# New prices in the list scheduler of an encoder-layer kernel

## The chip, the cores and the metric

The kernel runs on one core of a Trainium2 chip, as one program. The metric is the device time of one execution in microseconds (us). A core has TensorE (PE, matrix products), VectorE (DVE), ScalarE (ACT), GpSimd (POOL) and a queue that issues transfers (SP). Each engine takes its own instructions strictly in the order in which the program was written, and waits on semaphores for the others.

## The reference

One layer of a bidirectional encoder is applied to two sequences of 256 tokens, width 2048, with the same weights. Both are handled together, as 512 columns.

```
mod = silu(c) @ w_ada + b_ada            # six parts: shift, scale, gate, twice
h   = (rms_norm(x) * (1 + sc1) + sh1) @ w_in
# RWKV-7 group: 16 heads of 64, scanned once forward and once backward
S = S * w_t + (S @ -kk_t) b_t^T + v_t k_t^T ;  y_t = S @ r_t
# short-conv group: h_b * conv3(h_c * h_x)
x = x + gt1 * (concat(y_rwkv, y_conv) @ w_out)
f = rms_norm(x) * (1 + sc2) + sh2
x = x + gt2 * ((silu(f @ w_gate) * (f @ w_up)) @ w_down)     # 5632 wide
y = rms_norm(x)
```

## The kernel before, in words

**Products.** Every large product is made in three passes for accuracy: a weight block of 128x1024 arrives by DMA (`w`, three buffers), ACT copies half of it, rounded, into a tile `h` (four buffers), DVE subtracts to get the rest (`split`), and PE then makes, for each 128x128 tile, three matmuls of 128x512: high by high, high by low, low by high (`products`). One such triple is one node of the scheduler. Rows of the profile for these read `b<-r,h` or `b<-g,h`. `stream` runs through the tiles of one product. All matmuls are issued at line 374, PE's transposes at line 385, ACT's copies and activations at line 392, DVE's two-operand products at line 401, its scalar-and-tensor ones at line 406, its scans at 425, its own transposes at 437, and every DMA at line 434.

**Stages.** In the head, a first part of the adaLN weights and of `w_in` is loaded and multiplied. Then follow eight head pairs `p`. For each, `pre(p)` normalises keys and makes the low-rank products, gates and two scans; `core(p)` does the recurrence in chunks of 64 tokens; `fin(p)` normalises the heads' output. The `w_in` products of the following pair, and DVE's adaLN sums for later parts (`aacc<-aw`, priority 8), are the work that lies beside it; during the last pair it is half of `w_out`. After the pairs come the other half of `w_out`, the gate and up products, the down products and the last norm, nearly all of it 128x512 matmuls.

**The gram stage.** `core(p)` begins with decays (ACT), eight DVE products, and then four groups of small products, one for each direction `d` and half `q`: eight products with 64 rows, 128 weight columns and 128 columns of data, into two PSUM banks; banks 2 and 3 for `q` = 0, 4 and 6 for `q` = 1, so the third group needs the banks of the first and the fourth those of the second. Each pair of banks is emptied by six ACT copies of 32 rows (three per bank) and four DVE products (two per bank, one on 64 rows and one on 128). Two engines do not touch one bank at a time: ACT takes the first bank while DVE takes the second, then they change over. PE's transposes follow, into banks 2 to 4, then a triangular solve on DVE (31 steps, with DVE transposes around it and 32x32 products behind it) and four chunk steps in which PE, ACT and DVE take turns.

**What sets the order.** The whole layer is first noted down as nodes (`Program.add`): an engine, a price in us, a priority (small is urgent: splits 0, evictions 1, core 2, fin 3, pre 4, small sums 5, adaLN 8, wide products 9) and the nodes it depends on. `schedule` then plays through time: the engine that can start first takes its most urgent ready node; a node is ready when the nodes it depends on have ended and a `latency` between the two engines has passed. For a DMA the planned landing is issue, 0.65, its bytes at 360 GB/s, and 0.8. PE's prices are stretched where the played clock is cold. Nodes are issued in the order of their planned starts. So prices decide only which instruction stands ahead of which on each engine's queue; the time is the chip's own.

Of the kernel before, what the change touches and what calls it, by code (L numbers as in the profile page):

```python
# [196 lines left out]
class Program:  # L197
    SAME = {"pe": 0.0, "act": 0.145, "dve": 0.13, "pool": 0.12, "sp": 0.0}

    @classmethod  # L200
    def latency(cls, a, b):

        if a == b:
            return cls.SAME[a]
        return 0.3 if b == "pe" else 0.2 if a == "pe" else 0.14

    def __init__(self):
        self.nodes = []
# [2 lines left out]
    def add(self, eng, dur, fn, reads, writes, prio, table=None, nbytes=0, rows=1.0):  # L211
        i = len(self.nodes)
        deps = set()
        todo = [(x, False) for x in reads] + [(x, True) for x in writes]
        for x, w in todo:
            if not isinstance(x, (V, ScratchView)):
                continue
            vt, p0, p1, m = x.region()
            s = vt.slot
            if s.cur is not vt:  # L220
                deps.update(n for n, *_ in s.acc)
                s.acc = []
                s.cur, s.base = vt, i
            if s.base is not None:
                deps.add(s.base)
            keep = []
            for e in s.acc:
                n, q0, q1, k, ew = e
                if (w or ew) and q0 < p1 and p0 < q1 and k & m or s.psum and n < i and self.nodes[n][0] != eng:
                    deps.add(n)  # L230
                if not (w and p0 <= q0 and q1 <= p1 and (k & m) == k):
                    keep.append(e)
            keep.append((i, p0, p1, m, w))
            s.acc = keep
        deps.discard(i)
        self.nodes.append([eng, dur, fn, deps, prio, table, nbytes, self.hold, rows])
        return i

    def schedule(self):
# [24 lines left out]
        while done < n:  # L264
            best = None
            for e in engines:
                t = free[e]
                while pend[e] and pend[e][0][0] <= t:
                    _, i = heapq.heappop(pend[e])
                    heapq.heappush(avail[e], (nodes[i][4], i))  # L270
                if avail[e]:
                    s = t
                elif pend[e]:
                    s = pend[e][0][0]
                else:
                    continue
                if best is None or s < best[0]:
                    best = (s, e)
            s, e = best
            free[e] = max(free[e], s)  # L280
            while pend[e] and pend[e][0][0] <= s:
                _, i = heapq.heappop(pend[e])
                heapq.heappush(avail[e], (nodes[i][4], i))
            if e == "dve" and avail[e][0][0] >= LOOK_PRIO and pend[e]:
                soon = [r for r, j in pend[e] if r <= s + LOOK and nodes[j][4] <= 2]
                if soon:
                    free[e] = min(soon)
                    continue
            _, i = heapq.heappop(avail[e])
            if e == "pe" and not nodes[i][5]:  # L290

                busy = [x for x in busy if x[1] > s - WINDOW]
                if sum((x[1] - max(x[0], s - WINDOW)) * x[2] for x in busy) < LEAST * WINDOW:
                    wides = [x for x in avail[e] if nodes[x[1]][5]]
                    if wides:
                        heapq.heappush(avail[e], (nodes[i][4], i))
                        avail[e].remove(min(wides))
                        heapq.heapify(avail[e])
                        i = min(wides)[1]
            eng, dur, fn, deps, prio, tb, nbytes = nodes[i][:7]  # L300
            start[i] = s
            if e == "act" and tb is not None and table["act"] not in tb:
                dur += 1.3
                table["act"] = tb[0]
            if e == "pe":
                dur += 0.085 * bool(tb and not wide)
                wide = tb
                busy.append((s, s + dur, nodes[i][8]))
                t = s
                k = int(t // CLOCK_WINDOW)  # L310
                while win < k:
                    cold = used < COLD if not cold else used < HOT
                    win, used = win + 1, 0.0
                rest = dur
                while rest > 1e-9:
                    f = 2.0 if cold else 1.0
                    e2 = min(t + rest * f, (win + 1) * CLOCK_WINDOW)
                    used += (e2 - t) * nodes[i][8] / CLOCK_WINDOW
                    rest -= (e2 - t) / f
                    t = e2  # L320
                    if rest > 1e-9:
                        cold = used < COLD if not cold else used < HOT
                        win, used = win + 1, 0.0
                dur = t - s
            free[e] = s + dur
            end = s + dur
            if nbytes:
                dma_free = max(dma_free, end + 0.65) + nbytes / 360e3
                end = dma_free + 0.8
            order.append(i)  # L330
            done += 1
            for j in succ[i]:
                ready_at[j] = max(ready_at[j], end + self.latency(e, nodes[j][0]))
                left[j] -= 1
                if left[j] == 0:
                    heapq.heappush(pend[nodes[j][0]], (ready_at[j], j))
# [11 lines left out]
def hymba_layer_kernel(ctx: ExitStack, tc: tile.TileContext, xT, par, cst, w_ada0, w_ada1, w_in0, w_in1,  # L348
# [6 lines left out]
    def pe(mms, prio, after=()):  # L355


        def price(m):
            cols, n = m[1].idx.size, m[3]
            if m[6]:  # L360
                return max(cols / 1200.0, n / 2375.0)
            if cols > 64:
                return max(0.218, n / 597.0)
            if cols > 32:
                return max(0.081, 0.0277 + n / 1200.0)
            return max(0.037, 0.0205 + n / 2400.0, min(0.056, 0.03 + n / 2400.0))

        cost = sum(price(m) for m in mms)

        rows = sum((1 if m[6] else 4) * m[3] / 2400.0 * (m[1].p1 - m[1].p0) * m[1].idx.size  # L370
                   for m in mms) / (16384 * cost)

        def fn():
            return [nc.tensor.matmul(R(out), lhsT=R(l), rhs=R(r), start=start, stop=stop)  # L374
                    for out, l, r, n, start, stop, one in mms]
        add("pe", cost, fn, [m[1] for m in mms] + [m[2] for m in mms] + list(after), [m[0] for m in mms], prio,
            table=mms[0][6],
            rows=rows)
# [4 lines left out]
    def tr(items, prio):  # L383
        def fn():
            return [nc.tensor.transpose(R(out), R(i), R(idn)) for out, i, idn in items]  # L385
        add("pe", (0.003 + items[0][0].idx.size / 1200.0) * len(items), fn,
            [i[1] for i in items] + [items[0][2]], [i[0] for i in items], prio)

    def act(out, in_, func, n, prio, scale=1.0, bias=0.0):
        ex = [x for x in (scale, bias) if isinstance(x, V)]  # L390
        add("act", (0.05 if in_.vt.slot.psum else 0.095) + n / 1200.0 + 0.09 * len(ex),
            lambda: nc.scalar.activation(out=R(out), in_=R(in_), func=func, scale=R(scale), bias=R(bias)),  # L392
            [in_] + ex, [out], prio, table=TABLES.get(func))

# [2 lines left out]

    def tt(out, a, b, op, n, prio, eng="dve"):
        e = nc.vector if eng == "dve" else nc.gpsimd
        add(eng, 0.07 + n / 960.0 if eng == "dve" else 0.1 + n / 445.0,  # L400
            lambda: e.tensor_tensor(out=R(out), in0=R(a), in1=R(b), op=op), [a, b], [out], prio)  # L401

    def stt(out, a, s, b, op0, op1, n, prio, eng="dve"):
# [5 lines left out]
    def ts(out, a, s1, op0, n, prio, s2=None, op1=None, fast=True, eng="dve"):  # L409
        e = nc.vector if eng == "dve" else nc.gpsimd  # L410

        def fn():
            if s2 is None:
                return e.tensor_scalar(out=R(out), in0=R(a), scalar1=R(s1), scalar2=None, op0=op0)
            return e.tensor_scalar(out=R(out), in0=R(a), scalar1=R(s1), scalar2=R(s2), op0=op0, op1=op1)
        cost = 0.07 + n / (1920.0 if fast else 960.0) if eng == "dve" else 0.1 + n * 0.0036
        cost += 0.06 * (isinstance(s1, V) + isinstance(s2, V))
        add(eng, cost, fn, [a, s1, s2], [out], prio)

    def recip(out, a, n, prio):  # L420
# [1 line left out]
            lambda: nc.vector.reciprocal(out=R(out), in_=R(a)), [a], [out], prio)  # L422

    def scan(out, m, x, prio):
        add("dve", 0.62, lambda: nc.vector.tensor_tensor_scan(
            out=R(out), data0=R(m), data1=R(x), initial=0.0, op0=ALU.mult, op1=ALU.add), [m, x], [out], prio)

    def pset(out, val, n, prio):
# [5 lines left out]
        add(eng, cost, lambda: e.dma_start(R(out), R(in_)), [in_, *after], [out], prio, nbytes=nbytes)  # L434

    def tr32(out, in_, n, prio):
        add("dve", 0.07 + n / 960.0, lambda: nc.vector.transpose(R(out), R(in_)), [in_], [out], prio)  # L437

    S_SPLIT, S_EVAC, S_CORE, S_FIN, S_PRE, S_MISC, S_ADA, S_MAIN = 0, 1, 2, 3, 4, 5, 8, 9
    S_HEAD, S_REV = 2, S_CORE  # L440
# [965 lines left out]
```

## Time and profile before

| | us |
|---|---|
| median of 3 runs (lowest, highest) | 2571.69 (2567.66, 2575.66) |
| the profiled execution's own time | 2574.54 |
| its span, first to last instruction | 2572.8 |
| PE, PE weight load, DVE, ACT, POOL busy | 2495.1, 1992.2, 1490.0, 981.9, 12.0 |
| share of the chain that ended last: PE, DVE, DMA, ACT | 85%, 5%, 4%, 3% |

The profiled execution is one execution of its own, so its time differs a little from the median of the runs. A busy PE is not a PE at its peak: matmuls overlap, and the mean of one (396 ns for a 128x512) is longer than its distance to the next. In a row of the groups there stand line, engine, operation, output and inputs, shapes, count, then busy time, mean ns of one, and the idle time of the engine just before, with what ended it. In a row of the waits there stand who waited, for whom, the total in us, how often, and the longest.

### The profile page before, as it was taken

The numbers are of one execution on the slowest core, as the hardware profiler recorded it, in microseconds if no ns is written. First come the engines' busy times: TensorE is split into PE (matmuls) and PEld (weight loads), VectorE is DVE, ScalarE is ACT, GpSimd is POOL, SyncE is SP. The second block draws the span as 40 slices with busy tenths as digits, with TensorE's granted clock in tenths as the row PEclk, the third lists the DMA queues.
The fourth block names the chain that finished last, engine by engine and source line by source line (L and its number), as shares of the span: only waits on it lengthen the run. The fifth ranks groups of instructions, "written<-read, shape, count | busy, mean of one in ns | idle before, by whom it ended". The sixth has DMA issues, their size and how long they took to land.

```text
span 2572.8 us, 38989 instructions
## 1 busy us (share of the span) xinstructions
PE 2495.1 (97%) x15292; PEld 1992.2 (77%) x15292; DVE 1490.0 (58%) x2840; ACT 981.9 (38%) x1772; POOL 12.0 (0%) x42
## 2 busy tenths in 40 slices
PE   6999999999999999999999999999999999999997
PEld 3567677777777777798888888888888888888887
DVE  4268888888989886988743333333333333333345
ACT  4374655746636543433222222222222222222232
POOL 0000000000000000000000000000000000000000
PEclk9999999999999999999999999999999999999999
DMA  9953534545435658536643333333333333333333
GB/s 339 349 152 117 148 113 139 147 130 147 145 113 152 217 152 289 181 106 189 186 128 96 99 98 93 96 99 98 94 95 98 99 97 93 97 98 99 97 92 107
DMA packets 149033, 352.74 MB, mean 137 GB/s; under 512 B 31984, under 2 KB 46704, under 8 KB 148848
## 3 DMA queue, kind: packets, MB, share of 16 engines
q1 hardware_dynamic: 148848, 350.24, 43.7%
q8 instruction: 120, 1.97, 0.3%
q14 instruction: 65, 0.53, 0.1%
HBM read 339.30 MB, written 12.45 MB: 137 GB/s over the span
## 4 chain that ended last, share of the span: by engine, by line
PE 85%; DVE 5%; DMA 4%; ACT 3%; issue 1%; SPq 0%; DVEq 0%; ACTq 0%
PE b L374 85%; ACT g L392 2%; DVE g L401 2%; DMA aw<-in_w_ada_dram 2%; DVE aacc L406 1%; DVE h L401 1%; DVE g L406 1%; DMA g<-hrmean 1%; PE b L385 1%; DMA w<-in_w_in_dram 1%; SPq L434 0%; DMA g<-hrpre 0%; ACT h L392 0%; DMA hrmean<-rowm 0%; DVE g L437 0%
## 5 line engine op out<-in xcount | busy, mean ns | idle before, releaser
L374 PE MATMUL b<-r,h 128*128 128x512 f32 x4872 | 1189.1, 396 | 6.6 <-DVE h L401 2.6
L374 PEld LDWEIGHTS b<-r,h 128*128 128x128 f32 x4872 | 901.8, 189 | 227.4 <-issue 27.8
L374 PE MATMUL b<-g,h 128*128 128x512 f32 x4460 | 1043.6, 391 | 0.0
L374 PEld LDWEIGHTS b<-g,h 128*128 128x128 f32 x4460 | 836.5, 188 | 188.8 <-issue 9.6
L401 DVE TENSOR_TENSOR h<-w,h 128x512 fp32r<-128x512 f32 (+3 forms) x795 | 539.7, 681 | 748.4 <-ACT h L392 743.1
L392 ACT ACTIVATE h<-w 128x512 fp32r<-128x512 f32 x787 | 492.4, 627 | 1259.6 <-PE b L374 1219.6
L406 DVE SCALAR_TENSOR_TENSOR aacc<-aw,sil,aacc 128x512 f32<-128x512 f32 x420 | 299.1, 746 | 64.4 <-DMA aw<-in_w_ada_dram 63.1
L401 DVE TENSOR_TENSOR g<-g,g 128x512 f32<-128x512 f32 (+25 forms) x699 | 257.2, 375 | 35.5 <-ACT g L392 15.1
L392 ACT ACTIVATE g<-b 32x128 f32<-32x128 f32 (+4 forms) x441 | 175.1, 401 | 123.2 <-PE b L374 93.1
L374 PEld LDWEIGHTS b<-g,g 128*64 128x64 f32 (+4 forms) x4104 | 160.8, 141 | 72.1 <-ACT g L392 31.1
L374 PE MATMUL b<-g,g 128*64 128x64 f32 (+4 forms) x4104 | 182.5, 230 | 23.8 <-ACT g L392 20.4
L392 ACT ACTIVATE g<-g 128x512 f32<-128x512 f32 (+4 forms) x190 | 113.8, 601 | 78.0 <-DVE g L401 61.5
L406 DVE SCALAR_TENSOR_TENSOR r<-b,md,r 128x256 f32<-128x256 f32 x192 | 85.9, 480 | 88.2 <-PE b L374 87.9
L401 DVE TENSOR_TENSOR g<-g,b 128x512 f32<-128x512 f32 x60 | 41.2, 687 | 60.4 <-PE b L374 60.3
L392 ACT ACT_TABLE_LOAD x54 | 69.3, 1283 | 2.0 <-PEq L1395 0.7
L374 PE MATMUL b<-g,sil 128*32 128x512 f32 (+1 forms) x352 | 40.2, 552 | 19.5 <-DMA g<-in_w_ada_dram 18.7
L401 DVE TENSOR_TENSOR g<-b,cs 64x256 f32<-64x256 f32 (+1 forms) x128 | 50.3, 416 | 3.5 <-ACT g L392 2.4
L392 ACT ACTIVATE g<-r 128x512 f32<-128x512 f32 (+1 forms) x40 | 21.6, 542 | 51.7 <-DVE r L406 41.3
L437 DVE STREAM_TRANSPOSE g<-g 128x512 f32<-128x512 f32 (+1 forms) x32 | 37.7, 1205 | 0.2
L374 PEld LDWEIGHTS b<-g,sil 128*32 128x32 f32 x352 | 8.4, 113 | 35.2 <-ACT g L392 17.9
L385 PE MATMUL b<-cs,g 128*128 128x128 f32 x160 | 26.7, 308 | 8.8 <-ACT g L392 4.9
L385 PEld LDWEIGHTS b<-cs,g 128*128 128x128 f32 x160 | 21.2, 159 | 17.0 <-ACT g L392 12.2
(83 smaller groups left out, 562.0 us busy)
## 6 DMA issues: line engine op xcount, KB each, us to landing
w<-in_w_gu_dram SPq DMA_DIRECT2D x176, 512.0 KB
aw<-in_w_ada_dram SPq DMA_DIRECT2D x224, 256.0 KB
w<-in_w_in_dram SPq DMA_DIRECT2D x102, 512.0 KB
w<-in_w_down_dram SPq DMA_DIRECT2D x88, 512.0 KB
g<-in_w_ada_dram SPq DMA_DIRECT2D x72, 512.0 KB
w<-in_w_out_dram SPq DMA_DIRECT2D x32, 512.0 KB
g<-in_xT_dram SPq DMA_DIRECT2D x8, 512.0 KB
r<-in_xT_dram SPq DMA_DIRECT2D x16, 256.0 KB
```

The source lines that it names most:

```text
L374: return [nc.tensor.matmul(R(out), lhsT=R(l), rhs=R(r), start=start, stop=stop) for out, l, r, n, start, stop, one in mms]
L385: return [nc.tensor.transpose(R(out), R(i), R(idn)) for out, i, idn in items]
L392: lambda: nc.scalar.activation(out=R(out), in_=R(in_), func=func, scale=R(scale), bias=R(bias)),
L401: lambda: e.tensor_tensor(out=R(out), in0=R(a), in1=R(b), op=op), [a, b], [out], prio)
L406: lambda: e.scalar_tensor_tensor(out=R(out), in0=R(a), scalar=R(s), in1=R(b), op0=op0, op1=op1),
L437: add("dve", 0.07 + n / 960.0, lambda: nc.vector.transpose(R(out), R(in_)), [in_], [out], prio)
```

## The change

Only prices and latencies of the scheduler are replaced. No instruction, tile, buffer, priority or dependency is touched.

```diff
 def latency(cls, a, b):
-    return 0.3 if b == "pe" else 0.2 if a == "pe" else 0.14
+    return 0.18 if b == "pe" else 0.2 if a == "pe" else 0.13
 # schedule(), a PE node; tb: it is a triple of wide passes, wide: so was the one before
-    dur += 0.085 * bool(tb and not wide)
+    dur += 0.1 * bool(wide and not tb)
 # price of one matmul: cols weight columns, n columns of data, m[6]: one pass
-    return max(cols / 1200.0, n / 2375.0)
+    return n / 2400.0 + 0.0133
 if cols > 64:
-    return max(0.218, n / 597.0)
+    return 0.124 if m[1].p1 - m[1].p0 <= 64 else max(0.218, n / 597.0)
+def held(out):
+    return 0.1 * (out.p1 - out.p0 < 128)
 # act: (0.05 from PSUM, 0.095 from SBUF) + n / 1200 + 0.09 per column operand
+    ... + held(out)
 # tt on DVE: 0.07 + n / 960;  ts: 0.07 + n / 1920 or n / 960, + 0.06 per column operand
+    ... + held(out)
 # scan
-    0.62
+    1.13
 # tr32, DVE's transpose of 32x32 blocks
-    0.07 + n / 960.0
+    0.37 if n == 256 else 0.05 + n / 560.0
```

The first applies to all engines: the time from the end of a node to the earliest start of one that depends on it. `held` adds 0.1 to ACT copies, DVE two-operand products and DVE scalar operations whose output has fewer than 128 rows.

More of the change, by code (lines that the diff above doesn't have):

```diff
@@ L387, in tr @@
             [i[1] for i in items] + [items[0][2]], [i[0] for i in items], prio)
+    def held(out):
+        return 0.1 * (out.p1 - out.p0 < 128)
     def act(out, in_, func, n, prio, scale=1.0, bias=0.0):
         ex = [x for x in (scale, bias) if isinstance(x, V)]
-        add("act", (0.05 if in_.vt.slot.psum else 0.095) + n / 1200.0 + 0.09 * len(ex),
+        add("act", (0.05 if in_.vt.slot.psum else 0.095) + n / 1200.0 + 0.09 * len(ex) + held(out),
             lambda: nc.scalar.activation(out=R(out), in_=R(in_), func=func, scale=R(scale), bias=R(bias)),
@@ L399, in tt @@
         e = nc.vector if eng == "dve" else nc.gpsimd
-        add(eng, 0.07 + n / 960.0 if eng == "dve" else 0.1 + n / 445.0,
+        add(eng, 0.07 + n / 960.0 + held(out) if eng == "dve" else 0.1 + n / 445.0,
             lambda: e.tensor_tensor(out=R(out), in0=R(a), in1=R(b), op=op), [a, b], [out], prio)
@@ L416, in ts @@
         cost = 0.07 + n / (1920.0 if fast else 960.0) if eng == "dve" else 0.1 + n * 0.0036
-        cost += 0.06 * (isinstance(s1, V) + isinstance(s2, V))
+        cost += 0.06 * (isinstance(s1, V) + isinstance(s2, V)) + held(out)
         add(eng, cost, fn, [a, s1, s2], [out], prio)
@@ L424, in scan @@
     def scan(out, m, x, prio):
-        add("dve", 0.62, lambda: nc.vector.tensor_tensor_scan(
+        add("dve", 1.13, lambda: nc.vector.tensor_tensor_scan(
             out=R(out), data0=R(m), data1=R(x), initial=0.0, op0=ALU.mult, op1=ALU.add), [m, x], [out], prio)
@@ L436, in tr32 @@
     def tr32(out, in_, n, prio):
-        add("dve", 0.07 + n / 960.0, lambda: nc.vector.transpose(R(out), R(in_)), [in_], [out], prio)
+        add("dve", 0.37 if n == 256 else 0.05 + n / 560.0, lambda: nc.vector.transpose(R(out), R(in_)), [in_], [out], prio)
     S_SPLIT, S_EVAC, S_CORE, S_FIN, S_PRE, S_MISC, S_ADA, S_MAIN = 0, 1, 2, 3, 4, 5, 8, 9
```

## The prediction

> **What bounds the kernel now.** I read the page first, then the windows view, then the waits of TensorE, then the timeline at the places the waits name. The page and four stretches say where TensorE (PE) is not working:
>
> ```profile
> span 2572.8 us, 38989 instructions
> PE 2495.1 (97%) x15292; PEld 1992.2 (77%) x15292; DVE 1490.0 (58%) x2840; ACT 981.9 (38%) x1772; POOL 12.0 (0%) x42
> PEclk9999999999999999999999999999999999999999
> ```
> ```profile
> 0.00:150.00 150.00, 125.00 (x908) 72.29 (x909) 56.41 (x121) 62.81 (x110) 1.55 (x11) 0.98 0.86 317
> 150.00:1015.00 865.00, 826.01 (x7139) 640.92 (x7138) 753.51 (x1568) 482.61 (x939) 10.50 (x31) 0.98 0.50 151
> 1015.00:2560.00 1545.00, 1543.21 (x7244) 1278.35 (x7242) 672.74 (x1131) 436.25 (x722) 0.00 (x0) 1.00 0.37 111
> 2560.00:2573.00 13.00, 0.90 (x6) 0.63 (x5) 7.34 (x22) 0.20 (x1) 0.00 (x0) 0.62 0.49 162
> ```
>
> The columns are the stretch, its length, then busy time and count of PE, PEld, DVE, ACT and POOL, the granted clock, the DMA share and GB/s. PE is idle for 77.7 us of 2572.8: 25 in the head, 39 while the eight head pairs are scanned, 1.8 in the 1545 us after that, 12 at the end. An order cannot shorten what PE computes; it can only move these idle times, and the short ends of matmul runs. The head works at 317 GB/s and a DMA share of 0.86, so it is set by loads, and the last 13 us by a DVE chain. What the change can reach is the 39 us. Who is waited for there:
>
> ```profile
> PE b L374 <- ACT g L392: 23.7, 18, 4.2
> PE b L385 <- ACT g L392: 4.9, 5, 2.8
> PE b L385 <- DVE g L401: 3.3, 3, 1.4
> PE b L374 <- DVE g L401: 2.9, 5, 1.2
> PE b L374 <- DVE h L401: 2.6, 5, 1.6
> PE b L385 <- DVE g L406: 0.5, 2, 0.3
> ```
>
> These are 37.9 us in 38 waits. The largest item is PE waiting for ScalarE (ACT) copies out of PSUM. The timeline of one pair shows where (start, length, engine; in brackets the idle time before):
>
> ```profile
> 301.28 2.06 PE L374 MATMUL b<-g,g 64*128 64x128 f32 x32
> ...
> 302.53 0.83 ACT L392 ACTIVATE g<-b 32x128 f32<-32x128 f32 x3 [1.43 <-PE b L374]
> ...
> 303.27 0.97 PE L374 MATMUL b<-r,h 128*128 128x512 f32 x3
> ...
> 304.33 1.68 ACT L392 ACTIVATE g<-b 32x128 f32<-32x128 f32 x6 [0.97 <-DVE g L401]
> ...
> 305.28 1.16 PE L374 MATMUL b<-g,g 64*128 64x128 f32 x16 [1.05 <-ACT g L392]
> 305.71 1.64 DVE L401 TENSOR_TENSOR g<-b,cs 64x256 f32<-64x256 f32 x4
> 306.54 1.68 ACT L392 ACTIVATE g<-b 32x128 f32<-32x128 f32 x6 [0.53 <-PE b L374]
> ...
> 307.49 1.16 PE L374 MATMUL b<-g,g 64*128 64x128 f32 x16 [1.05 <-ACT g L392]
> 308.58 0.97 PE L374 MATMUL b<-r,h 128*128 128x512 f32 x3
> ...
> 309.28 0.75 DVE L406 SCALAR_TENSOR_TENSOR g<-g,pm 128x512 f32<-128x512 f32 x1 [1.93 <-DMA g<-hrvar]
> ...
> 312.39 1.07 PE L385 MATMUL b<-cs,g 128*128 128x128 f32 x8 [2.84 <-ACT g L392]
> ```
>
> This is the gram stage of core(p): four groups of 8 small products (two records each: 16), whose banks are emptied by 6 ACT copies and 4 VectorE (DVE) products each, then the transposes. The third and fourth group reuse the banks of the first and second. PE stands still 1.05 us before each, and between them the order has nothing else for it. Waits of another kind, outside this stage or behind a landing DMA, are these:
>
> ```profile
> 251.06 1.12 PE L374 MATMUL b<-g,g 128*64 128x64 f32 x26 [2.38 <-ACT g L392]
> ```
> ```profile
> 404.01 0.69 DVE L406 SCALAR_TENSOR_TENSOR g<-g 128x512 f32<-128x512 f32 x1 [1.35 <-DMA g<-hrmean]
> ...
> 406.41 2.08 PE L374 MATMUL b<-g,g 64*128 64x128 f32 x16 [2.44 <-ACT g L392]
> ```
> ```profile
> 606.77 0.63 ACT L392 ACTIVATE h<-w 128x512 fp32r<-128x512 f32 x1 [3.78 <-DMA w<-in_w_in_dram]
> ...
> 610.43 3.78 PE L374 MATMUL b<-g,g 64*128 64x128 f32 x32 [4.17 <-ACT g L392]
> ```
> ```profile
> 1011.32 0.43 PE L374 MATMUL b<-g,cs 128*32 128x64 f32 x16 [1.25 <-ACT g L392]
> ```
>
> With the one at 312.39 they are 2.84 + 2.38 + 2.44 + 4.17 + 1.25 = 13.1 us. Taking these and the 2.6 us for DVE h from 37.9 leaves 22 us, 2.8 us for each of 8 pairs, for gram stages.
>
> **The change part by part.** No instruction is added or removed; queues keep their work in another order. The rows that the new prices are to be held against:
>
> ```profile
> L392 ACT ACTIVATE g<-b 32x128 f32<-32x128 f32 x192 | 51.5, 268 | 26.3 <-DVE g L401 16.4 <-PE b L374 7.3
> L392 ACT ACTIVATE g<-b 128x256 f32<-128x256 f32 x32 | 12.1, 380 | 17.2 <-PE b L374 10.9 <-DVE g L401 6.2
> L401 DVE TENSOR_TENSOR g<-b,cs 64x256 f32<-64x256 f32 x64 | 26.7, 417 | 3.1 <-ACT g L392 2.4
> L425 DVE TENSOR_TENSOR_SCAN g<-cmask,g 128x512 f32<-128x512 f32 x16 | 19.4, 1214 | 0.6 <-ACT g L392 0.6
> L437 DVE STREAM_TRANSPOSE g<-g 128x512 f32<-128x512 f32 x24 | 21.7, 940 | 0.2
> ```
>
> *Gram products (price) and short evictions (held).* A group was priced 8 x 0.218 = 1.74 us, and is now 8 x 0.124 = 0.99, plus 0.1 behind a wide product; the timeline has 1.16. An ACT copy of 128 columns out of PSUM was 0.05 + 128/1200 = 0.157 and is now 0.257; the timeline has 1.68/6 = 0.28. A DVE product on 64 rows was 0.337 and is 0.437; the timeline has 1.64/4 = 0.41 over both kinds. So the old plan saw PE occupied 0.6 us too long per group and the eviction ended too early, and both errors hide the hole. By hand, old plan: groups end at 1.74 and 3.49; the first pair of banks is emptied (0.2 to the reader, three copies 0.47, 0.2, two products 0.67) at 3.3 and usable at 3.6, so one product node (three matmuls) goes between; the second pair of banks is ready while the third group runs, so nothing goes before the fourth. That is the order of the rows at 301.28 to 307.49. New plan by the same working: groups end at 1.09 and 2.08; the banks are emptied (0.2, 0.77, 0.13, 0.77) at 2.96, usable at 3.14; product nodes at 2.08 and 2.76 end at 3.44. The third group ends at 4.53; the second pair of banks, whose copies queue behind the first's, is usable at about 4.8, so another node goes in, to 5.2; the transposes again get one node before them. So two further product nodes, six matmuls, move into each gram stage.
>
> What they are worth comes from the steady rate and the run of three:
>
> ```profile
> 1500.00:1550.00 50.00, 50.00 (x222) 41.44 (x221) 15.06 (x22) 13.62 (x22) 0.00 (x0) 1.00 0.33 98
> ```
>
> 222 matmuls of 128x512 in 50 us are 0.225 us each, so six are 1.35 us of work that need not be done later. A run of three takes 0.97 in the timeline instead of 0.68: a run that is new costs up to 0.29. The first node lengthens a run, the second makes a new one: 1.35 - 0.29 = 1.06 us per pair at least, 2.8 us if every gram wait went. I take 1.5, near the lower end, because a wait of 1.05 is filled by whole nodes of 0.68 and the wait before the transposes keeps its one node. 8 x 1.5 = 12 us (bounds 8.5 and 22). Are there products to put in? ACT, which splits the weights, waits for PE far more than for weights in this stretch, so split tiles lie ready:
>
> ```profile
> ACT h L392 <- PE b L374: 185.4, 118, 3.0
> ...
> ACT h L392 <- DMA w<-in_w_in_dram: 3.8, 1, 3.8
> ```
>
> *Wide products (price).* 512/2375 = 0.2156 becomes 0.2266; the steady row gives 0.225. The plan had 288 such matmuls in a pair's 96 tiles 3 us too short, so PE ran late against its plan, a margin that is now gone. It costs nothing where a core step is late on PE; it exposes other errors, counted below. The Trainium skill's page TensorE: Matmul & The Clock Gate (section Back-to-back issue gap) puts the gap of N = 512 at 518 cycles, 216 ns, which is the old price. By it the new plan would count 3 us of filler per pair that PE does not have, more than the 1.5 won, and the sum would be no change; the row's 222 in 50 us, and not 231, speaks for the new price.
>
> *Scan 0.62 to 1.13, transposes 0.60 to 0.96 (512) and 1.14 to 1.88 (1024).* These are late steps of pre and core that the old plan started too early, by about 1 and 2.2 us a pair. What waits for scans is the first gram group: the 2.9 us for DVE g hold all of it. I take 1 us as won (bounds 0 and 2.9). Transposes release the 32x32 products, and no large wait names them: nothing, covered by the wide products; if the cover were gone it would be 8 x 2.2 = 18 us, and the old order, not the new one, has that risk.
>
> *Latency to PE 0.3 to 0.18, others 0.14 to 0.13, 0.1 for wide to small.* Every group that PE takes from another engine is set up to 0.12 us earlier. In the timeline the 3rd of the 6 copies from 304.33 ends near 305.17 and PE starts at 305.28: 0.11, inside the new 0.18. The 128x256 copy is the exception, priced 0.263 + 0.18 = 0.44 against 0.380 + 0.11 = 0.49, so PE may stand 0.05 us at each: 4 per pair, 1.6 us; bounds 0 and, if all of a pair's small groups (33 by the code: grams 4, transposes 5, head sums 4, the four steps 18, the 32x32 products 2) lost the whole 0.12, 32. I take 1, by the measured 0.11.
>
> *DMA landings, SP and POOL.* Their prices stay. Loads and the row spreads are reordered on SP with the work that asks for them; the 13.1 us above are left as they are (bounds 0 and double, since a DVE queue stopped by a landing holds back whatever was put behind it). Head and tail: loads and a DVE chain set them, 0 (bounds -2 and +2). The feed-forward stretch has 1.8 us idle: 0.
>
> Sum: -12 - 1 + 1 = -12 us on the profiled execution of 2574.5 us (span 2572.8), which gives 2562.5. That execution lay 2.8 us over the median of 2571.7, so against the median it is about 2560.
>
> **Rivals.** *The same time (2568 to 2574).* The products pulled forward are missing later: the core's chain through DVE and ACT sets a pair's period and PE's wait only moves. For it: DVE is busy 753.5 of 865 us there, and landings stop it. Against: PE is busy 826 of 865, so a chain that PE does not set would have to be within 5% of PE's own work. If 10 of the 12 us come back, 2570.
>
> *Slower, by the margin taken off.* The place is each small group released by ACT or DVE, most of all the four-step loop at the end of core: with 0.12 less allowed per edge, PE stands before groups that now arrive just in time. 8 pairs x 33 groups = 264; the whole 0.12 on each is +32, less the 12 won, gives 2592; half is 2576. It decides from 0.075 us per group (+20). For it: the 380 ns row. Against: the 0.11 us measured.
>
> *It does not do what it says.* Evictions are priced right, but a DVE filler (weights of adaLN) or a split stands ahead of them in the queue, so the order of the gram stage or its waits stay: 2572.
>
> **How the numbers follow.** Filled gram stages 0.57; wait only moved 0.22; unchanged stages 0.08; margin lost 0.13. The three runs of before differ by 8 us, 0.3%, so 0.3% (7.7 us) is what a measurement can tell. Of the first case about 0.02 falls short of it and the margin case may end within it or beyond: faster 0.56, same 0.29, slower 0.15. The low end, 2547, is all 22 us of gram waits plus a few us of landings; the high end, 2576, is the unmoved time plus 4 us of lost margin. The likeliest case alone spans 2552 to 2565.
>
> **What would show it.** After: between the second and third 16-record group of a gram stage six wide matmuls instead of three, and a run of three between the third and fourth; PE waiting for ACT g in the pairs' stretch near 12 us instead of 23.7, with PE busy time within 5 us of 2495 and the span less by the wait that went. Wrong if the idle total of that stretch stays at 39 us, if new waits stand before the 128x64 products, or if waits behind landings grow from 13 to over 20 us.

## The result, and the profile after

The changed kernel took 2590.78 us (median of 4 runs, 2585.09 to 2591.28), the kernel before 2573.68 on the same chips (2567.66 to 2576.05): a ratio of 1.0065, interval 1.0041 to 1.0088. A later set of runs gave 2587.01 against 2568.57, 1.0066 (1.0051 to 1.0081). It is slower by 0.65%, where 0.45% faster was forecast. Lines of the helpers have moved down by four (ACT L396, DVE L405 and L410), here and in every kernel that has the new prices of ACT and DVE.

The page, with the one group of TensorE that is new among the costly ones, and the windows view for the same four stretches as before:

```profile
span 2583.3 us, 39000 instructions
PE 2490.0 (96%) x15292; PEld 1991.3 (77%) x15292; DVE 1489.9 (58%) x2840; ACT 969.2 (38%) x1763; POOL 12.5 (0%) x42
...
L374 PE MATMUL b<-aacc,cs 128*32 128x128 f32 x224 | 10.6, 290 | 25.8 <-DVE aacc L410 25.8
```
```profile
0.00:150.00 150.00, 123.34 (x908) 71.79 (x909) 59.10 (x125) 62.37 (x110) 1.55 (x11) 0.99 0.87 319
150.00:1015.00 865.00, 848.22 (x7297) 659.76 (x7295) 754.17 (x1574) 482.12 (x950) 10.96 (x31) 1.00 0.51 154
1015.00:2560.00 1545.00, 1508.39 (x7013) 1250.17 (x7010) 661.62 (x1102) 422.87 (x698) 0.00 (x0) 0.99 0.36 108
2560.00:2590.00 30.00, 10.10 (x82) 9.61 (x80) 15.00 (x42) 1.85 (x5) 0.00 (x0) 0.80 0.43 141
```

In the pairs' stretch PE's idle time fell from 39 us to 16.8, by more than the 12 us forecast. Between 1015 and 2560 us it rose from 1.8 to 36.6. The rest is small: PE's busy time fell by 5.1 us, idle time in head and tail rose by 3.0. The sum, -22.2 + 34.8 + 3.0 - 5.1, is the 10.5 us between the two spans.

The waits of PE in the pairs' stretch, after:

```profile
PE b L385 <- DVE g L405: 5.4, 2, 3.1
PE b L374 <- ACT g L396: 3.7, 5, 1.3
PE b L374 <- DVE g L441: 3.2, 3, 1.6
```

The waits for ACT's evictions fell from 23.7 + 4.9 us to 3.7 + 0.2. One gram stage in the timeline, next to the one at 301 us of before:

```profile
285.81 1.28 PE L374 MATMUL b<-g,g 64*128 64x128 f32 x20
...
287.03 2.34 PE L374 MATMUL b<-r,h 128*128 128x512 f32 x9
...
289.30 1.16 PE L374 MATMUL b<-g,g 64*128 64x128 f32 x16
...
290.39 0.97 PE L374 MATMUL b<-r,h 128*128 128x512 f32 x3
...
291.28 1.16 PE L374 MATMUL b<-g,g 64*128 64x128 f32 x16
...
292.38 1.65 PE L374 MATMUL b<-r,h 128*128 128x512 f32 x6
...
293.87 1.04 PE L385 MATMUL b<-cs,g 128*128 128x128 f32 x8
```

Nine wide matmuls stand before the third group (three before the change), three between the third and fourth (none before), six before the transposes (three before), and no row has an idle time. So the gram stage was refilled as the prediction's hand working said, with one node more in two places. Over all eight stages the rows of the gram products had 20.5 us of idle time before and have 1.7 now. Counted in the trace, PE had made 3051 wide matmuls of 128x512 by 1015 us, against 2909 before. At the second norm it then ran out of work. PE at the second norm, after the change and before it:

```profile
1089.78 1.36 PE L374 MATMUL b<-r,g 128*128 128x256 f32 x10
1112.91 1.32 PE L374 MATMUL b<-aacc,cs 128*32 128x128 f32 x16 [21.77 <-DVE aacc L410]
1114.80 1.01 PE L374 MATMUL b<-cs,g 128*128 128x1 f32 x4 [0.57 <-DVE asum L441]
1119.01 1.22 PE L374 MATMUL b<-cs,rs 128*128 128x128 f32 x4 [3.19 <-DVE rs L405]
1121.51 3.78 PE L374 MATMUL b<-r,g 128*128 128x256 f32 x14 [1.28 <-ACT r L396]
```
```profile
1107.11 2.28 PE L374 MATMUL b<-r,g 128*128 128x256 f32 x18
1109.32 0.64 PE L374 MATMUL b<-aacc,cs 128*32 128x128 f32 x16
1109.90 1.31 PE L374 MATMUL b<-r,g 128*128 128x256 f32 x9
1111.05 0.50 PE L374 MATMUL b<-cs,g 128*128 128x1 f32 x4
```

The row with `aacc` adds up the partitions of the adaLN sum of group 9, which DVE makes as its least urgent work. It came at 1109.32 before and at 1112.91 after, nearly the same time. Before, PE was still busy when it came: the last operation of the sum had ended at 1108.45, 0.9 us ahead. After, PE had been standing for 21.8 us, and behind it in PE's queue stood the mean squares of the second half of the norm (the 128x1 row), whose own chain then cost another 5 us. What DVE did meanwhile, from the chain of waits after:

```profile
1097.01 2.55 DMA aw<-in_w_ada_dram
1099.61 0.04 issue
1099.65 1.43 DVE aacc L410 x2
1101.10 2.63 DMA aw<-in_w_ada_dram
1103.73 0.03 issue
1103.78 0.04 issue
1103.82 1.43 DVE aacc L410 x2
```

It went back and forth between a landing of 256 KB and two operations. From 1087.3 us on it did nothing else; the whole group took 35 us, from 1077.9 to 1112.9, with work for the first half of the norm in the first part of that time. The sums were behind before this stretch began: of their DVE operations (32 for a group) 278 had been made by 1015 us before the change and 254 after it, though DVE was busy for as long in the pairs' stretch (753.5 and 754.2 us).

### The profile page after: what moved, and what is told of

Same layout as the page of the kernel before. It is cut to its first block, busy times and chain, and to the rows that moved or that the text cites. A ratio compares the mean times of both kernels' runs of the same rounds, so it can differ in the third digit from the quotient of the medians.

```text
span 2583.3 us, 39000 instructions
## 1 busy us (share of the span) xinstructions
PE 2490.0 (96%) x15292; PEld 1991.3 (77%) x15292; DVE 1489.9 (58%) x2840; ACT 969.2 (38%) x1763; POOL 12.5 (0%) x42
## 4 chain that ended last, share of the span: by engine, by line
PE 66%; DVE 7%; DMA 6%; ACT 2%; issue 2%; SPq 0%; DVEq 0%; ACTq 0%
PE b L374 66%; DMA aw<-in_w_ada_dram 4%; DVE aacc L410 2%; DVE g L405 2%; DVE h L405 1%; ACT g L396 1%; DVE g L410 1%; DMA g<-hrvar 1%; ACT h L396 0%; DVE r L410 0%; ACT L396 0%; DMA g<-hrmean 0%; DMA g<-hrpre 0%; DMA g<-yc 0%; DMA r<-in_w_ada_dram 0%
## 5 line engine op out<-in xcount | busy, mean ns | idle before, releaser
L405 DVE TENSOR_TENSOR h<-w,h 128x512 fp32r<-128x512 f32 (+3 forms) x795 | 540.4, 681 | 765.2 <-ACT h L396 737.1
L396 ACT ACTIVATE h<-w 128x512 fp32r<-128x512 f32 x787 | 492.7, 627 | 1227.1 <-PE b L374 1185.4
L410 DVE SCALAR_TENSOR_TENSOR aacc<-aw,sil,aacc 128x512 f32<-128x512 f32 x420 | 297.2, 746 | 82.1 <-DMA aw<-in_w_ada_dram 81.3
L405 DVE TENSOR_TENSOR g<-g,g 128x512 f32<-128x512 f32 (+24 forms) x699 | 256.4, 375 | 33.7 <-ACT g L396 11.6
L396 ACT ACTIVATE g<-b 32x128 f32<-32x128 f32 (+4 forms) x441 | 175.1, 401 | 133.4 <-PE b L374 103.3
L396 ACT ACTIVATE g<-g 128x512 f32<-128x512 f32 (+3 forms) x190 | 113.6, 601 | 62.8 <-DVE g L405 50.9
L410 DVE SCALAR_TENSOR_TENSOR r<-b,md,r 128x256 f32<-128x256 f32 x192 | 85.1, 480 | 56.9 <-PE b L374 56.9
L405 DVE TENSOR_TENSOR g<-g,b 128x512 f32<-128x512 f32 x60 | 41.0, 686 | 58.4 <-PE b L374 58.4
L405 DVE TENSOR_TENSOR g<-b,cs 64x256 f32<-64x256 f32 (+1 forms) x128 | 49.7, 417 | 1.6
L396 ACT ACTIVATE g<-r 128x512 f32<-128x512 f32 (+1 forms) x40 | 21.7, 543 | 63.0 <-DVE r L410 51.2
L374 PEld LDWEIGHTS b<-g,sil 128*32 128x32 f32 x352 | 8.4, 113 | 37.8 <-ACT g L396 17.6
L374 PE MATMUL b<-aacc,cs 128*32 128x128 f32 x224 | 10.6, 290 | 25.8 <-DVE aacc L410 25.8
L396 ACT ACTIVATE g<-g,md 128x256 f32<-128x256 f32 (+1 forms) x48 | 25.4, 562 | 19.2 <-DVE md L405 14.2
```

What stands on the lines that cost most here:

```text
L410: lambda: e.scalar_tensor_tensor(out=R(out), in0=R(a), scalar=R(s), in1=R(b), op0=op0, op1=op1),
```

## The experiments

**Is the wait for group 9 the loss?** Theory A: yes. Theory B: the loss is the margin taken off. Group 9 was given to PE, as groups 10 and 11 are already, in the new kernel and, as a control, in the old one.

```diff
-ADA_AT = ((0, 1, 2), (3, 4), (5,), (6,), (7,), (8,), (9,), ())
-ADA_PE, ADA_LATE = (10, 11), (12, 13, 14, 15)
+ADA_AT = ((0, 1, 2), (3, 4), (5,), (6,), (7,), (8,), (), ())
+ADA_PE, ADA_LATE = (9, 10, 11), (12, 13, 14, 15)
```

New kernel, expected: 

> The new order with one thing changed: the adaLN group 9, whose weighted sum DVE makes in the new and the old kernel, is made by PE like groups 10 and 11 (32 small matmuls, 3.64 us in the old trace at 1048 to 1052, and 8 loads). Theory A (the gram waits are filled as forecast, PE gets ahead of DVE, and the gain and more is given back in the single wait of 21.8 us for the sum of group 9 ahead of the second norm): the wait goes, 4 us of PE are added, so 2591 - 22 + 4 = 2573 or a little less, and the waits of PE for aacc fall from 25.8 to under 8 us. Theory B (the loss is the margin taken off: many small waits): nothing but the 4 us, 2595.

Old kernel, expected: 

> The old order with the same move of group 9 to PE, as a control. Theory A: the old order has no PE wait for a DVE sum in front of the second norm, so there is nothing to win and the 4 us are paid: 2574 to 2578. Theory B: the same. If this gains as much as the run above, the move is good for a reason of its own and tells nothing of the change.

Measured: the new kernel 2554.10 us, ratio to the kernel before 0.9945 (0.9930 to 0.9960); the old one 2574.46, 1.0022 (1.0012 to 1.0032). The first waits of PE, whole run, of the new kernel with the move:

```profile
PE b L374 <- DMA g<-in_w_ada_dram: 18.6, 2, 17.3
PE b L385 <- DVE g L405: 5.8, 2, 3.6
PE b L374 <- DVE g L405: 5.0, 6, 1.5
PE b L374 <- ACT g L396: 3.7, 5, 1.1
PE b L374 <- DVE aacc L410: 3.4, 2, 2.9
```

Theory A holds, and it expected too little: not 18 us but 33 to 37 came off. PE's busy time is the same (2490.5 us), so it is all idle time. From 1015 us to the end the idle time fell by 30: 22.4 us of it are waits for `aacc` (25.8 became 3.4, and these stand before group 8), the rest is part of the norm's chain. The old kernel paid 4.6 us, the price of the move, and won nothing. So, against the kernel before, the prices and the move together were good for 16 us.

**Which half of the prices is it?** PE's prices with the latencies, and ACT's and DVE's, each alone on the old kernel.

```diff
 # pe_prices_only: latency, wide to small, wide product, gram product as in the change
 # vector_prices_only: held(), scan, tr32 as in the change
```

> Old prices with the PE half of the change alone: wide product, wide to small, gram products, latency. ACT and DVE prices (short outputs, scan, transposes) stay old. Theory A: the phantom PE time of the gram stage is gone, so about half of the 22 us of gram waits are filled, and DVE keeps the sums as early as before; the sum of group 9 still ends near 1110 us, so little of it can arrive at the end: 2565 to 2575. Theory B: shorter latency and exact products are the whole loss: 2590 or more.

> Old prices with the ACT and DVE half alone: short outputs, scan, transposes. Theory A: DVE and ACT are planned fuller, core steps later, so adaLN sums, the least urgent work of DVE, slide back as in the new kernel, PE pulls products forward and waits ahead of the second norm: 2580 to 2595, PE waiting for aacc over 10 us. Theory B: no margin is taken off PE here, so the gram waits are filled for nothing: 2560 to 2570.

Measured: 2585.32 us, 1.0064 (1.0039 to 1.0089), and 2589.72, 1.0079 (1.0064 to 1.0094). Each half alone costs as much as both. PE's waits, first with PE's prices, then with ACT's and DVE's:

```profile
PE b L374 <- DVE g L401: 18.7, 9, 3.6
...
PE b L374 <- ACT g L392: 9.3, 15, 1.8
```
```profile
PE b L374 <- DVE aacc L410: 20.5, 3, 19.5
...
PE b L374 <- DVE g L405: 13.2, 11, 3.3
PE b L385 <- ACT g L396: 8.6, 7, 3.0
```

The ACT and DVE half is as Theory A said: the sum comes at 1122.2 and PE stands 19.5 us before it. The PE half fits neither expectation: PE has no wait for group 9 in front of the norm and reaches its row at 1117.4. In the pairs it is idle for 40 us as before the change, but waits for DVE's core products in place of ACT's evictions. Its span is 13 us longer than that of the kernel before, 6 us of it more busy time of PE and 7 us more idle time; what makes the busy time longer was not settled.

**Is DVE's time short, or the order bad?** Three runs on the new kernel: the sum of group 9 cut to a quarter in its place (12 of its 16 row blocks are left out); the sums 5 to 9 sooner; groups 8 and 9 both on PE.

```diff
 # after_sum9_cut
-            for kk in range(KT):
+            for kk in range(4 if gi == 9 else KT):
 # after_sums_sooner: priority of the sums' DVE work and loads
-        ps = bank[5 if slots is None else 6]
+        ps, S_ADA = bank[5 if slots is None else 6], 7 if 5 <= gi <= 9 else 8
 # after_sums89_on_pe, with a fourth set of slots for the loads
-ADA_AT = ((0, 1, 2), (3, 4), (5,), (6,), (7,), (8,), (9,), ())
-ADA_PE, ADA_LATE = (10, 11), (12, 13, 14, 15)
+ADA_AT = ((0, 1, 2), (3, 4), (5,), (6,), (7,), (), (), ())
+ADA_PE, ADA_LATE = (8, 9, 10, 11), (12, 13, 14, 15)
```

> The new order with group 9 still summed by DVE into the same bank and the same place, but over 4 of its 16 row blocks: 12 blocks, their 24 DVE operations and 12 loads are left out. Theory A1 (what is short is DVE time for the sums: 24 x 0.67 = 16 us of DVE and some landing waits): the wait of 21.8 us goes without any work for PE, 2590 - 22 - 10 = 2550 to 2560, as the run with the sum on PE less its 4 us. Theory A2 (it is the bank that the sum shares with the second half of the norm, or its place in PE's queue, that costs): group 9 still stands there and the time stays over 2580.

> The new prices with the adaLN sums 5 to 9 at priority 7 in place of 8, so that DVE no longer holds back for a core operation about to be ready and makes these sums sooner; same instructions. Theory A1 (before the second norm DVE's work, and not its order, is the bound): the wait for aacc shrinks, but the core's steps come later by as much, and PE waits in the pairs instead: 2580 to 2595. Theory A3 (only the order is bad; the sums could be had for nothing): the wait goes, 2555 to 2570.

> The new order with groups 8 and 9 both summed by PE. With group 9 moved PE waited 3.4 us for aacc and the time was 2554. Theory A1: DVE is the bound no longer after the first move, so the second adds 4 us of PE work and wins at most the 3 us that are left: 2553 to 2558. If DVE still were the bound, another 21 us of its work less would show: 2540 to 2548.

Measured: 2558.12 us (0.9959, 0.9938 to 0.9979), 2580.98 (1.0050, 1.0029 to 1.0072) and 2553.45 (0.9938, 0.9917 to 0.9959). In the run with the cut, group 9 has the same bank and the same place and costs PE no wait:

```profile
1083.92 0.77 PE L374 MATMUL b<-aacc,cs 128*32 128x128 f32 x16
```

With the sums made sooner group 9 is ready at 1035 us, 78 us earlier, and the time is only 6 to 10 us less than that of the new kernel, with intervals that overlap. The pairs' stretch shows where it went:

```profile
PE b L374 <- ACT g L396: 25.3, 18, 5.1
PE b L374 <- POOL g L433: 8.3, 1, 8.3
```
```profile
150.00:1015.00 865.00, 821.04 (x7129) 642.07 (x7128) 761.33 (x1594) 466.67 (x926) 10.84 (x31) 0.97 0.52 158
```

PE's idle time in the pairs is back at 44 us. So with these prices it is DVE's time ahead of the second norm, with its waits for landings, that is short, and making the sums sooner only moves the place where PE stands. (That no order could do better is not shown: a run below keeps all these sums on DVE and takes 2560 us.) All three runs came as Theory A1 said. With both groups on PE nothing more is won: after one, DVE does not bound this stretch any more.

**What of the margin?** The old latencies in the new kernel, with group 9 on PE and without, the new ones in the old kernel, and both moves of groups with old latencies.

```diff
-        return 0.18 if b == "pe" else 0.2 if a == "pe" else 0.13
+        return 0.3 if b == "pe" else 0.2 if a == "pe" else 0.14
```

> The new prices with group 9 on PE, but the latencies of before (0.3 to PE, 0.14 between others). Theory B in its small form (0.12 less allowed for each edge makes PE stand before groups that come just in time): with the margin back 3 to 8 us are won, 2546 to 2551. Without it: within 3 us of 2554.

> The new kernel with the latencies of before alone put back; group 9 stays on DVE. With group 9 on PE the old latency won 7 us. Theory A: DVE's sums still bound the way to the second norm, so what PE wins in the pairs is waited for there: 2580 to 2590, with PE waiting 15 to 25 us for aacc. If the latency were the main loss of the change: 2565 to 2575.

> The old kernel with the new latencies alone. If 0.12 us less for each edge to PE costs by itself, as the 7 us of the earlier pair of runs says: 2575 to 2580. If it costs only beside exact prices: 2568 to 2572.

> The new prices with old latencies and groups 8 and 9 on PE: the two moves that won, together. If they add up: 2546 or a little less; DVE is not the bound any more, so at most 3 us less than with group 9 alone (2547), and 4 us of PE work more.

Measured: 2546.86 us (0.9908, 0.9891 to 0.9925), 2568.33 (0.9991, 0.9981 to 1.0001), 2572.54 (1.0007, 0.9994 to 1.0021) and 2550.26 (0.9921, 0.9902 to 0.9941). The first has the lowest median of this study, 0.9% under the kernel before; its interval overlaps that of the last. The new latencies do nothing to the old kernel that can be measured. In the new one they cost 7 us with group 9 on PE, 3 us (within the intervals) with groups 8 and 9 there, and about 20 with both on DVE. This last was a miss of Theory A, which expected 2580 to 2590 and had a wait of 15 to 25 us right (18.5). The last run of the four came 4 us over the 2546 that would have shown the two moves adding up. Three further runs asked whether the size of the latency decides, or the accident of an order; a fourth repeated the new kernel beside them.

> The new kernel with 0.3 again to PE, 0.13 between the others. Theory M (margin to PE: what is released to PE later is filled with wide products, and DVE's sums are not put behind core steps): nearly all of the 22 us are back, 2566 to 2572. Theory S (scatter of a greedy order): anywhere from 2560 to 2592, not near 2568 in particular.

> The new kernel with 0.14 again between ACT, DVE, POOL and SP, 0.18 to PE. Theory M: nothing, 2586 to 2594. Theory S: 0.01 us in a price moves the time by 5 us or more, either way.

> The new kernel with 0.24 to PE, half way. Theory M: between the ends, 2575 to 2582. Theory S: outside of them.

> The new kernel itself, on the chip of the three others: 2585 to 2592, with which they are to be compared.

Measured: 0.30 to PE 2570.56 us (1.0003, 0.9993 to 1.0013); 0.14 between the others 2575.62 (1.0022, 1.0012 to 1.0032); 0.24 to PE 2559.87 (0.9961, 0.9946 to 0.9976); the new kernel again 2587.01. The run with 0.30 came where Theory M put it. But the middle value is faster than both ends, and 0.01 us in the price of an edge is worth 11 us; Theory M has neither, and Theory S, scatter, has both. The scatter has largely one place. PE's row for group 9 with 0.24 to PE, and with the old latencies:

```profile
1089.37 1.32 PE L374 MATMUL b<-aacc,cs 128*32 128x128 f32 x16 [11.67 <-DVE aacc L410]
```
```profile
1099.91 1.32 PE L374 MATMUL b<-aacc,cs 128*32 128x128 f32 x16 [16.47 <-DVE aacc L410]
```

The same row in every kernel whose group 9 is summed in full by DVE at the old priority:

| kernel | DVE busy, 150 to 1015 us | group 9's row on PE starts | PE idle just before it | span | span less the start | median |
|---|---|---|---|---|---|---|
| to PE 0.24 | 767.8 | 1089.4 | 11.7 | 2558.3 | 1468.9 | 2559.9 |
| old latencies | 759.7 | 1099.9 | 16.5 | 2566.4 | 1466.5 | 2568.3 |
| others 0.14 | 756.6 | 1101.4 | 22.4 | 2571.4 | 1470.0 | 2575.6 |
| to PE 0.30 | 762.5 | 1101.5 | 18.0 | 2570.9 | 1469.4 | 2570.6 |
| before, new latencies | 757.2 | 1106.8 | 0 | 2568.7 | 1461.9 | 2572.5 |
| before | 753.5 | 1109.3 | 0 | 2572.8 | 1463.5 | 2573.7 |
| changed kernel | 754.2 | 1112.9 | 21.8 | 2583.3 | 1470.4 | 2590.8 |
| PE prices only | 747.7 | 1117.4 | 0 | 2586.0 | 1468.6 | 2585.3 |
| vector prices only | 746.2 | 1122.2 | 19.5 | 2587.8 | 1465.6 | 2589.7 |

The row starts over a range of 33 us; what follows it takes 1462 to 1470 us everywhere. In six of the kernels PE stood before the row and was released by the end of DVE's sum, so there the moment at which DVE ends group 9 sets the time, and by and large it is early where DVE is busy for more of the pairs' stretch. In the three others PE came to the row with its own work and waited for nothing; for these the table does not say that DVE's sum sets the time. The old kernel and the changed one differ by 3.6 us in the start of the row and by 6.9 in what follows it, where the norm's chain and the later groups make PE wait. Which of DVE's waits makes the sum late in a given order was not settled. The waits for landings of row spreads do not explain it: `hrvar`, `hrpre` and `hrmean` held DVE for 19.6 us in that stretch in the changed kernel and 8.4 with 0.24 to PE, but 24.4 with 0.14 between the others, whose sum ended 11.5 us before that of the changed kernel.

**How much of the gain is the ACT and DVE half's?** That half alone on the old kernel, with group 9 on PE (the first diff of this section).

> Old prices with the ACT and DVE half of the change, and group 9 on PE. The ACT and DVE half alone took 2590, with 20.5 us of PE waiting for aacc. Theory A: these go for 4 us of PE work, 2560 to 2570, and what is left to the 2547 to 2554 of the full change is the PE half's share (gram products and exact wide products).

Measured: 2567.36 us, 0.9978 (0.9967 to 0.9989), as expected. With group 9 out of the way this half is worth 7 us against the control's 2574.5, the whole change 20, the whole change without its latencies 28.

## Why the prediction was wrong

*Gram products and short evictions: the mechanism right, the value not.* PE's waits for ACT in the pairs fell by 25 us and its idle time by 22, more than the 12 taken, by the nodes named and one more in two places. Two waits that the prediction left among the landings, 2.44 and 4.17 us, stood before gram products and went as well. (A slip in the hand working, 0.2 from ACT to DVE in the old plan where the list has 0.14, changes nothing in it.) The step that failed is "1.35 us of work that need not be done later". That holds only if PE, once ahead, need not stop for another engine later. It had to, between 1091 and 1113 us, 21.8 us before the row of group 9. The signs named under "What would show it" could not catch this: all that would have counted as wrong lay in the pairs' stretch and did not come (16.8 us of idle time there in all), and the loss lay behind it.

*The rival nearest to what came was rejected by an average.* "DVE is busy 753.5 of 865 us" against "PE is busy 826 of 865" was read as 5% of room for PE. Busy time left out that DVE's adaLN chain alternates with landings (the waits for `aw` were 37.8 us of that stretch before, and the spreads' came on top), and that it has a due time: two groups must be in before the second norm. The rival put the returned wait in the pairs, on the core's chain, and let 10 of 12 us come back. It came back at the norm, on the sums' chain, 22 us, and took the norm's small chain and the later groups' waits with it: 36.6 us idle where 1.8 had been.

*DVE fillers were costed at nothing.* In the new order the adaLN sums fall back behind other work of DVE (254 operations by 1015 us against 278; group 8 reaches PE at 1076.8 against 1038.4), and the prediction named nobody who waits for them. PE does, at one row, with the norm behind it. Nothing in this scheduler's priorities says when a piece of low priority is due. That the old, too low prices of ACT's and DVE's work had left planned room for the sums fits the two halves (257 operations by 1015 us with the ACT and DVE half, 278 with the PE half), but the plan itself was not looked at. This is the term that was missing from the sum.

*Wide products:* the steady rate is unchanged (221 in 1500 to 1550 us against 222) and PE's busy time moved by 5.1 us, close to the 5 said. *Scan and transposes:* 1 us forecast; not tried alone. *Latency:* 1 us forecast. It is 0 in the old kernel, 7 in the relieved new one, and about 20 in the changed kernel, where it acts mostly through the end of group 9 (13 us earlier with the old latencies) and not, as the slower rival had it, by waits at 264 small groups. It does not grow with the latency taken off, as the run with 0.24 shows. *Landings:* left at 13 us; what became of the others of these waits was not separated.

*The range* was made from PE's waits alone, and so its slow end, 2576, stood for lost margin alone. The time lay 15 us beyond it.

## What to carry to other kernels

Prices nearer to the trace make a greedy scheduler fill the holes it can see, and they can also push an engine's least urgent work back; look up when that work is due before counting a filled hole as a gain. When an engine gets ahead, find in the trace the first instruction at which it must stop for another, and ask when that one is ready now: here the row of one sum, at 1109 us, was ready 0.9 us before PE came to it, which would have said that PE's 22 us could not be kept. If small, unrelated price changes move a time by 10 us either way, look for the one event whose moment the time follows, and relieve that (here one group of 16 moved to PE: 33 to 37 us).

## What the runs showed of the hardware

A weighted sum whose weights came through one tile of two halves was bound by landings even while DVE did nothing else: from 1087.3 to 1113.5 us of the changed kernel DVE made 13 pairs of operations of 1.42 us, 18.5 us of work in 26.3, and stood 0.15 to 1.07 us before each pair after the first for a landing. From the end of the operations on a half to the landing of its next 256 KB the chain of waits shows 2.45 to 2.92 us. The same order repeats well (2585 to 2591 us in two sets of four runs), so the differences of 10 to 20 us between nearly equal price lists belong to the orders.
